# Two load buffers for the modulation weights, and a fourth for the blocks of w1, in a two-layer diffusion backbone

## The chip, the cores and the metric

The kernel runs on one core of one Trainium2 chip, as one launch. The metric is the device time of that launch in microseconds, the median of several runs. The engines of the core are TensorE (PE, with PEld for its weight loads), VectorE (DVE), ScalarE (ACT), GpSimd (POOL) and SyncE (SP), which issues nearly all DMAs here. The profile is one execution of the program; its clock starts at the first instruction.

## The reference, cut to what matters

512 latent tokens and 256 context tokens of width 1024 go through two layers. Each layer is a modulated norm, a mixer (Fourier, latent attention, convolution) with an output projection, and a squared-ReLU MLP of width 4096:

```python
def channel_mlp(h, l):
    return jnp.square(jax.nn.relu(h @ w_mlp1[l])) @ w_mlp2[l]

for l in range(DEPTH):
    last = l == DEPTH - 1
    mx = jnp.split((silu_c @ w_mod[l] + b_mod[l])[:, None, :], N_MOD, axis=-1)
    mc = jnp.split(silu_cc @ w_mod[l] + b_mod[l], N_MOD, axis=-1)
    ...
    if not last:
        ...
        hc = modulate(rms_norm(ctx, norm2_g[l]), mc[3], mc[4])
        ctx = ctx + mc[5] * channel_mlp(hc, l)
    x = x + mx[2] * mixer_rest(fx, gx, attn_x, l)
    hx = modulate(rms_norm(x, norm2_g[l]), mx[3], mx[4])
    x = x + mx[5] * channel_mlp(hx, l)
return rms_norm(x, final_norm_g)
```

The modulation (`mx` for the latent tokens, `mc` for the context) is a product of one vector with a 1024 x 6144 matrix for each layer and each of the two vectors. It doesn't depend on the tokens, so it can be worked out at any time before it is used. The change touches where the weights of that product are loaded while the MLP of layer 0 runs. The diff and the code call that layer 0 (`l == 0`); it is the first of the two, "layer one" in some speech.

## The kernel before, in words

**Products.** Activations lie with features on the 128 partitions and tokens on the free axis. Each fp32 operand is split in a high and a low part, and each product is three matmuls (`mm3`: high x high, high x low, low x high). Weights come by DMA into a raw buffer (tag `raw`), ACT makes the high part, and POOL or DVE subtracts to get the low part (`load_w`, tag `hl`, for whole 128 x 1024 tiles; `block`, tag `hs`, for 128 x 512 halves).

**The MLP.** Six of the 32 tiles of the hidden width are done plainly (`first_pairs`). The other 26 are done as 13 pairs (`pair(p)`, p = 3 to 15), whose latent part is a fast 2 x 2 scheme with seven half-size products (numbered 1, 6, 5, 7, 2, 3, 4 in the order of issue) in place of eight; the context part is four plain products. The sums of weight blocks that the scheme needs are DVE operations (L1183 to L1186), the sums of the products too (L1211), and then comes squared ReLU (L1169, L1044). After each pair, two blocks of w2 are multiplied with earlier hidden tiles: `downs` is called twice (j = 0 and j = 1), each with four output tiles mi = 0 to 3, and each output tile ends in an `update` (L983: one DVE operation for the latent part `resx`, one for the context part `resc`), which adds it to the residual. So one step of the loop in layer 0 is a pair and eight output tiles. PSUM holds three tiles for these in rotation (`ps` two, `pv` one) and two smaller ones (`tr`).

**The modulation.** Layer 0's last 8 groups of 128 outputs and all 48 of layer 1 are worked out on DVE during layer 0's MLP: `mod_group` loads 128 x 1024 weights (512 KB) into a buffer `w`, and one DVE reduce for each vector (`mj`, L274, with a short accumulator read behind it) multiplies it with the broadcast vector `c` and sums it. Layer 1's groups 0 to 15 need both vectors, so two reduces; groups 16 to 47 need one. Eight groups are spent in `first_pairs`; the other 48 are spent in the last call of `downs` of each step, four to a step in 12 steps: one ahead of the update of mi = 1, one ahead of that of mi = 2 and two ahead of that of mi = 3 (in the first of the steps, one, two and one). The first 16 of these 48 groups are the ones with two reduces. All 48 use one and the same buffer: `acc`, which is otherwise the accumulator of squares for the norms (and holds sums of `make_forms` early in the MLP).

**Order.** Each engine has one queue, in an order that is fixed when the program is built. The builder goes by the order in which the source emits instructions, but lets a later one pass where, by its own estimate of durations, an earlier one still lacks its inputs or its buffer. `tc.issue_after(mark[0])` keeps a reduce behind the DVE operation marked last (an update or a ReLU). So the reduces don't lie in the queues where the source emits them. A DMA that needs a buffer waits in SP's queue for the buffer's last reader, and everything behind it on SP waits too.

**Buffers.** Pool `ml` holds `raw` (128 x 1024 fp32, 4 KB on each partition, three buffers), `hs` (four of 4 KB) and `sw` (one of 6 KB). `raw` serves the blocks of w1 in both layers (`load_pair`), and by `wcfg` the tiles of the output projection and of the first tiles of w1. A pair takes two of the three. Pools are stacked in SBUF: after `ml` come, in layer 0, the broadcast vector `cb`, the buffers of the output projection's modulation (`mq`, `mr`, `mw`), and then the MLP's input `h2`.

Of the kernel before, what the change touches and what calls it, by code (L numbers as in the profile page):

```python
# [10 lines left out]
F32 = mybir.dt.float32  # L11
# [7 lines left out]
P = 128  # L19
D = 1024  # L20
# [54 lines left out]
def body(tc, A, out):  # L75
    nc = tc.nc
# [7 lines left out]
    def nm(s):  # L84
        cnt[0] += 1
        return f"{s}{cnt[0]}"

    def pool(name, **kw):
        cm = tc.tile_pool(name=nm(name), bufs=1, **kw)
        p = cm.__enter__()  # L90
        return p, lambda: cm.__exit__(None, None, None)

    cst, cst_close = pool("cst")
    wp, wp_close = pool("wp")
# [48 lines left out]
    wcfg = {"raw": [(wp, 2)], "hl": [(wp, 2)], "i": 0}  # L143
# [124 lines left out]
    def mod_group(o, w, l, g, nv=2):  # L268

        p, c, _ = o  # L270
        SY.dma_start(w, A["wmodT"][l, g])
        j = p.tile([P, D], BF16, tag="mj", name=nm("mj"), bufs=1)
        for v in range(nv):
            V.tensor_tensor_reduce(j, w, c[:, v], 1.0, vc("bmod", l, g), ALU.mult, ALU.add, mod[l][v][:, g:g + 1])  # L274
# [668 lines left out]
    for l in range(DEPTH):  # L943
# [7 lines left out]
        if l == 0:  # L951
            rx, rx_close = pool("rx")
            acc = rx.tile([P, D], F32, name="acc")
# [10 lines left out]
            load_res(0)  # L964
            load_res(1)
        ml, ml_close = pool("ml")
        wcfg.update(raw=[(ml, 3)], hl=[(wp, 2)], i=0)
        mods = None
        if l == 0:
            mods = open_mods()  # L970
# [8 lines left out]
        def update(pt, m, gate, cols, first, l=l):  # L979
            o0 = cols[0][0]  # L980
            for a, b, v in cols:
                r = res[v][m][:, a - S * v:b - S * v]
                mark[0] = V.scalar_tensor_tensor(r, pt[:, a - o0:b - o0],  # L983
                                                 mod[l][v][:, gate * 8 + m:gate * 8 + m + 1], r, ALU.mult, ALU.add).ins
                if first == "last":
                    sq_last[a, b] = tmp(b - a)
                    SC.activation(sq_last[a, b], r, AF.Square)
                elif first is not None:
                    add_square(acc[:, a:b], r, first)
# [58 lines left out]
        def more_mods(w):  # L1048
            ll, g = todo.pop(0)
            with tc.issue_after(mark[0]):  # L1050
                mod_group(mods, w, ll, g, 2 if ll == 0 or g < 16 else 1)
# [5 lines left out]
            return w  # L1057

        def load_pair(p, i):
            raw = ml.tile([P, 2, 512], F32, tag="raw", name=nm("raw"), bufs=3)  # L1060
            SY.dma_start(raw, A["w1"][l, 2 * p + i].rearrange("p (k n) -> p k n", k=2))
            return raw

        def load_tile(j):

            e = FIRST_W[l][j]
            if FIRST_AT[l][j] == "h":
                w = load_w(A["w1"][l, j], 1024, eng=e)
                return [w[:, :, 0:512], w[:, :, 512:1024]]
            raw = load_pair(j // 2, j % 2)  # L1070
            return [block(raw[:, i], e) for i in range(2)]
# [32 lines left out]
        def down(tiles, jobs, cols):  # L1104

            o0, nk = cols[0][0], len(tiles)
            os = sums_for(len(jobs), cols[-1][1] - o0)
            for (w, mi), o in zip(jobs, os):
                for k, ht in enumerate(tiles):
                    r = slice(k * (1024 // nk) + mi * P, k * (1024 // nk) + mi * P + P)  # L1110
                    mm3([(o[:, a - o0:b - o0], ht[:, 0, a:b], ht[:, 1, a:b]) for a, b, _ in cols],
                        w[:, 0, r], w[:, 1, r], k == 0, k == nk - 1)
            return os
# [59 lines left out]
        def pair(p):  # L1173


            ctx = not last
            r1, r2 = load_pair(p, 0), load_pair(p, 1)
            sw = ml.tile([P, 3, 512], F32, tag="sw", name=nm("sw"), bufs=1)
            hid[2 * p], hid[2 * p + 1] = ht = [unit(), unit()]
# [43 lines left out]
        def downs(ts, w, j, n):  # L1223
            for mi, o in enumerate(o for i in range(n) for o in down(ts, [(w, i)], whole)):
                if mods and len(hid) >= 8:
                    for _ in range(MODS[len(hid) > 8][j * n + mi]):
                        if todo:
                            more_mods(acc)
                update(o, j * n + mi, 5, whole, None)

        def load_down(j):
# [26 lines left out]
        for st in steps:  # L1258
            if isinstance(st, int):
                pair(st)  # L1260
                continue
            c, j = st
            for _ in range(plan.pop(0) if plan else 0):
                make_forms(made)
                made += 1
            ts = tiles(4 * c, 4) if last else tiles(2 * c, 2)
            downs(ts, ahead.pop(0) if ahead else load_down(8 // nd * c + j), j, nd)
# [179 lines left out]

# [10 lines left out]
```

## Time and profile before

| | |
|---|---|
| median of 3 runs | 1619.68 us |
| the runs | 1611.36, 1622.63, 1619.68 us |
| the profiled execution | 1613.05 us, span 1611.3 us |
| TensorE's mean granted clock | 0.983 of full speed |

The span is the time from the first to the last instruction on the core, so 1.75 us of the profiled execution lie around it. The profiled execution is 6.6 us shorter than the median of the runs, and the runs lie 11 us apart.

### The profile page before, as it was taken

The page shows a single profiled execution, that of the slowest core. Times are in us where ns is not written, and L with a number is a line of the kernel's source. Part 1 is how long each engine was busy: PE and PEld are TensorE (multiplying, and loading weights), DVE is VectorE, ACT ScalarE, POOL GpSimd, SP SyncE. Part 2 cuts the span into 40 slices and gives each one's busy share as a digit, 9 for nine tenths or more (in the row PEclk, how much of TensorE's full clock was granted, in tenths as well). Part 3 has the DMA queues.
Part 4 walks back from the last instruction along what each step waited for, and adds up shares of the span by engine and source line. Part 5 has one row for each costly group of instructions (what it writes and reads, how often), then busy time and mean ns, then how long its engine had stood idle before and what let it go on. Part 6 is the DMA issues. An engine that isn't in the chain of part 4 may idle for free.

```text
span 1611.3 us, 24743 instructions
## 1 busy us (share of the span) xinstructions
PE 1512.9 (94%) x9524; PEld 1322.3 (82%) x9524; DVE 1210.0 (75%) x1967; ACT 697.9 (43%) x1291; POOL 663.3 (41%) x440
## 2 busy tenths in 40 slices
PE   5998998899999999999999999899999989999997
PEld 3698877788888888889999987777878778888997
DVE  3489678867798899877877869978866676666655
ACT  3343577742423332333333244268854434444442
POOL 0034234212324554444454332443325566666671
PEclk9999999999999999999999999999999989999999
DMA  8331111066322333334333323100023122223321
GB/s 286 118 127 34 60 60 59 1 231 214 131 68 90 105 105 118 118 125 150 119 106 133 116 92 114 36 27 26 32 78 106 60 86 88 94 93 105 106 79 66
DMA packets 51142, 159.55 MB, mean 99 GB/s; under 512 B 5808, under 2 KB 13776, under 8 KB 50512
## 3 DMA queue, kind: packets, MB, share of 16 engines
q1 hardware_dynamic: 50592, 152.69, 28.7%
q0 software_dynamic: 432, 5.28, 0.8%
q8 instruction: 75, 1.23, 0.3%
q14 instruction: 43, 0.35, 0.1%
HBM read 155.84 MB, written 2.11 MB: 98 GB/s over the span
## 4 chain that ended last, share of the span: by engine, by line
PE 57%; DVE 22%; issue 6%; ACT 5%; DMA 5%; POOL 3%; DVEq 0%; SPq 0%; POOLq 0%; ACTq 0%
PE ps L160 30%; PE pv L160 15%; PE tr L160 6%; DVE mj L274 4%; DMA acc<-in_wmodT 3%; DVE aw L751 2%; ACT p L842 2%; DVE ac L751 2%; DVE resx L983 2%; PE tr L858 2%; PE po L160 1%; POOL hl L156 1%; PE tr L288 1%; PE p L160 1%; DVE t L1139 1%
## 5 line engine op out<-in xcount | busy, mean ns | idle before, releaser
L160 PE MATMUL ps<-y,hl 128*128 128x512 f32 (+1 forms) x2004 | 408.6, 356 | 8.2 <-DVE resc L983 3.8
L160 PEld LDWEIGHTS ps<-y,hl 128*128 128x128 f32 x2004 | 325.5, 189 | 70.5 <-DVE resc L983 7.5
L156 POOL TENSOR_TENSOR hl<-raw,hl 128x1024 fp32r<-128x1024 f32 (+1 forms) x90 | 223.4, 2483 | 252.2 <-ACT hl L155 252.1
L160 PE MATMUL pv<-y,hl 128*128 128x512 f32 (+1 forms) x1032 | 212.3, 355 | 1.9 <-DVE resc L983 1.7
L155 ACT ACTIVATE hl<-raw 128x1024 fp32r<-128x1024 f32 (+2 forms) x94 | 98.0, 1045 | 241.2 <-PE pv L160 112.2
L160 PEld LDWEIGHTS pv<-y,hl 128*128 128x128 f32 x1032 | 167.9, 188 | 34.2 <-DVE resc L983 3.1
L1056 POOL TENSOR_TENSOR hs<-raw,hs 128x512 fp32r<-128x512 f32 x95 | 133.2, 1404 | 125.2 <-ACT hs L1055 125.1
L160 PE MATMUL ps<-h,hs 128*128 128x256 f32 (+1 forms) x1080 | 151.4, 293 | 4.2 <-DVE t L1211 2.2
L1055 ACT ACTIVATE hs<-raw 128x512 fp32r<-128x512 f32 x133 | 82.9, 630 | 155.0 <-DMA raw<-in_w 42.3
L160 PEld LDWEIGHTS ps<-h,hs 128*128 128x128 f32 x1080 | 140.4, 193 | 10.1 <-issue 2.4
L983 DVE SCALAR_TENSOR_TENSOR resx<-ps,mod,resx 128x512 f32<-128x512 f32 (+1 forms) x134 | 95.6, 718 | 46.6 <-PE ps L160 46.6
L274 DVE CUSTOM_DVE_ANT_0 mj<-acc,cb,vec 128x1024 bf16<-128x1024 f32 x64 | 102.5, 1602 | 35.9 <-DMA acc<-in_wmodT 35.6
L1163 POOL TENSOR_TENSOR y<-t,y 128x256 fp32r<-128x256 f32 (+1 forms) x78 | 73.5, 956 | 113.6 <-DVE t L1169 110.0
L179 POOL TENSOR_TENSOR sm<-sm,mhalf 128x2 f32<-128x2 f32 (+2 forms) x16 | 17.7, 1109 | 193.8 <-DVE sm L177 193.8
L160 PE MATMUL tr<-h,hs 128*128 128x256 f32 x624 | 84.0, 285 | 0.0
L862 DVE TENSOR_TENSOR pT<-tr,pT 128x384 fp32r<-128x384 f32 (+1 forms) x144 | 74.0, 533 | 9.7 <-ACT pT L861 9.1
L861 ACT ACTIVATE pT<-tr 128x384 fp32r<-128x384 f32 (+1 forms) x144 | 65.8, 477 | 34.6 <-PE tr L858 33.5
L858 PE MATMUL tr<-ident,p 128*128 128x128 f32 x416 | 69.3, 281 | 11.1 <-DVE pT L862 7.0
L160 PEld LDWEIGHTS tr<-h,hs 128*128 128x128 f32 x624 | 79.3, 193 | 0.6
L983 DVE SCALAR_TENSOR_TENSOR resx<-pv,mod,resx 128x512 f32<-128x512 f32 (+1 forms) x75 | 54.0, 722 | 34.1 <-PE pv L160 33.9
L160 PE MATMUL pv<-h,hs 128*128 128x256 f32 (+1 forms) x504 | 77.4, 303 | 2.3 <-DVE h L225 2.3
L160 PEld LDWEIGHTS pv<-h,hs 128*128 128x128 f32 x504 | 69.4, 194 | 6.1 <-DVE h L225 2.7
(283 smaller groups left out, 2941.0 us busy)
## 6 DMA issues: line engine op xcount, KB each, us to landing
raw<-in_w SPq DMA_DIRECT2D x128, 512.0 KB, 3.6
acc<-in_wmodT SPq DMA_DIRECT2D x48, 512.0 KB, 3.5
mq<-in_wmods SPq DMA_DIRECT2D x32, 512.0 KB, 7.0
raw<-in_wo SPq DMA_DIRECT2D x17, 512.0 KB, 4.5
ztab<-in_dftx POOLq DMA_DIRECT2D x2, 2064.0 KB, 9.8
mw<-in_wmodT SPq DMA_DIRECT2D x8, 512.0 KB, 5.1
y<-in_wmodT SPq DMA_DIRECT2D x8, 512.0 KB, 5.5
raw<-in_win SPq DMA_DIRECT2D x8, 448.0 KB, 4.0
```

Of the source, the lines that this page charges most:

```text
L155: SC.activation(w[:, 0], raw, AF.Copy)
L156: side[eng].tensor_tensor(w[:, 1], raw, f(w[:, 0]), ALU.subtract)
L160: PE.matmul(o, lhsT=l, rhs=r, start=start, stop=stop)
L274: V.tensor_tensor_reduce(j, w, c[:, v], 1.0, vc("bmod", l, g), ALU.mult, ALU.add, mod[l][v][:, g:g + 1])
L751: V.scalar_tensor_tensor(acw[ct], us[ct][:, i:i + wide], vc("wdw", l, ct * TAPS + i), acw[ct], ALU.mult, ALU.add)
L858: PE.transpose(tr[:, (kt - ka) * P:(kt - ka + 1) * P], ptiles[i][:, kt * P:kt * P + P], ident)
L861: SC.activation(d[:, 0], src, AF.Copy)
L862: V.tensor_tensor(d[:, 1], src, f(d[:, 0]), ALU.subtract)
L983: mark[0] = V.scalar_tensor_tensor(r, pt[:, a - o0:b - o0], mod[l][v][:, gate * 8 + m:gate * 8 + m + 1], r, ALU.mult, ALU.add).ins
L1055: SC.activation(w[:, 0], src, AF.Copy)
L1056: side[eng].tensor_tensor(w[:, 1], src, f(w[:, 0]), ALU.subtract)
L1163: GP.tensor_tensor(ht[:, 1, a:a + n], src, f(ht[:, 0, a:a + n]), ALU.subtract)
```

## The change

Three things change. In `downs`, `mod_group` gets a tile of its own (tag `mw` in pool `ml`, two buffers of 4 KB on each partition) in place of `acc`. The tag `raw` of pool `ml` has four buffers in place of three, in both layers and for both users of the tag. The space that the build sets aside in SBUF for the descriptors of DMAs issued by GpSimd is halved, from 4096 to 2048. The pool `ml` grows by 4 KB in layer 1 and by 12 KB in layer 0, so what is stacked above it moves up by as much.

```diff
--- before.py
+++ after.py
@@ -964,7 +964,7 @@
             load_res(0)
             load_res(1)
         ml, ml_close = pool("ml")
-        wcfg.update(raw=[(ml, 3)], hl=[(wp, 2)], i=0)
+        wcfg.update(raw=[(ml, 4)], hl=[(wp, 2)], i=0)
         mods = None
         if l == 0:
             mods = open_mods()
@@ -1057,7 +1057,7 @@
             return w
 
         def load_pair(p, i):
-            raw = ml.tile([P, 2, 512], F32, tag="raw", name=nm("raw"), bufs=3)
+            raw = ml.tile([P, 2, 512], F32, tag="raw", name=nm("raw"), bufs=4)
             SY.dma_start(raw, A["w1"][l, 2 * p + i].rearrange("p (k n) -> p k n", k=2))
             return raw
 
@@ -1225,7 +1225,7 @@
                 if mods and len(hid) >= 8:
                     for _ in range(MODS[len(hid) > 8][j * n + mi]):
                         if todo:
-                            more_mods(acc)
+                            more_mods(ml.tile([P, D], F32, tag="mw", name=nm("mw"), bufs=2))
                 update(o, j * n + mi, 5, whole, None)
 
         def load_down(j):
@@ -1447,7 +1447,7 @@
 
 def kernel(**inputs):
     ins = _layout({k: np.asarray(v) for k, v in inputs.items()})
-    nc = bacc.Bacc("TRN2", target_bir_lowering=False, num_devices=1, dynamic_dma_scratch_size=4096)
+    nc = bacc.Bacc("TRN2", target_bir_lowering=False, num_devices=1, dynamic_dma_scratch_size=2048)
     aps = {n: nc.dram_tensor(f"in_{n}", a.shape, F32, kind="ExternalInput").ap() for n, a in ins.items()}
     out = nc.dram_tensor("out_y", (P, KT, S), F32, kind="ExternalOutput").ap()
     with tile.TileContext(nc) as tc:
```

## Rows read from the trace of the kernel before

**Rows 1.** The page: busy time, share of the span and instructions of each engine.

```profile
PE 1512.9 (94%) x9524; PEld 1322.3 (82%) x9524; DVE 1210.0 (75%) x1967; ACT 697.9 (43%) x1291; POOL 663.3 (41%) x440
```

**Rows 2.** Windows, one MLP step each: length, engines' busy time (instructions), clock, DMA, GB/s.

```profile
537.24:573.60 36.36, 33.47 (x230) 30.46 (x229) 33.06 (x51) 11.17 (x20) 16.85 (x11) 1.00 0.33 115
573.60:609.34 35.74, 33.47 (x231) 30.44 (x230) 32.28 (x52) 11.24 (x20) 17.52 (x11) 1.00 0.37 118
609.34:645.27 35.93, 33.46 (x231) 30.44 (x229) 32.41 (x52) 11.24 (x20) 17.50 (x11) 1.00 0.36 117
645.27:681.56 36.29, 33.78 (x230) 30.46 (x229) 32.87 (x52) 11.23 (x20) 17.52 (x11) 1.00 0.37 122
681.56:718.48 36.92, 34.56 (x230) 32.02 (x229) 27.55 (x43) 11.22 (x20) 14.88 (x11) 0.95 0.36 121
718.48:751.21 32.73, 32.73 (x230) 30.42 (x229) 26.06 (x43) 11.12 (x20) 15.25 (x11) 1.00 0.40 128
```

**Rows 3.** Timeline of PE: start, length, matmuls, [idle before, releaser].

```profile
651.01 1.59 PE L160 MATMUL pv<-y,hs 128*128 128x256 f32 x12
...
659.88 1.66 PE L160 MATMUL ps<-y,hs 128*128 128x256 f32 x12 [1.54 <-DVE t L1211]
...
670.07 2.38 PE L160 MATMUL ps<-y,hl 128*128 128x512 f32 x12 [0.77 <-DVE resc L983]
...
692.90 2.35 PE L160 MATMUL ps<-h,hs 128*128 128x256 f32 x12 [2.22 <-DVE t L1211]
695.05 2.45 PE L160 MATMUL tr<-h,hs 128*128 128x256 f32 x12
```

**Rows 4.** Timeline of DVE around the pair that starts at 645.27.

```profile
640.81 1.27 DVE L274 CUSTOM_DVE_ANT_0 mj<-acc,cb,vec 128x1024 bf16<-128x1024 f32 x1
...
642.67 1.27 DVE L274 CUSTOM_DVE_ANT_0 mj<-acc,cb,vec 128x1024 bf16<-128x1024 f32 x1
...
646.14 0.47 DVE L983 SCALAR_TENSOR_TENSOR resc<-pv,mod,resc 128x256 f32<-128x256 f32 x1
647.59 2.51 DVE L274 CUSTOM_DVE_ANT_0 mj<-acc,cb,vec 128x1024 bf16<-128x1024 f32 x1 [0.98 <-DMA acc<-in_wmodT]
...
656.57 1.28 DVE L274 CUSTOM_DVE_ANT_0 mj<-acc,cb,vec 128x1024 bf16<-128x1024 f32 x1 [2.34 <-DMA acc<-in_wmodT]
```

**Rows 5.** Waits between 537.24 and 718.48: who for whom, total, times, longest.

```profile
DVE mj L274 <- DMA acc<-in_wmodT: 16.7, 11, 2.5
```

**Rows 6.** Timeline of SP over the same step: DMA issues.

```profile
652.99 0.33 SPq L271 DMA_DIRECT2D acc<-in_wmodT  x1
653.41 2.00 SPq L1061 DMA_DIRECT2D raw<-in_w  x2
```

**Rows 7.** The tile `acc`: times from its DMAs' issue to their landing.

```profile
DMA to landing us min/median/max: 3.3/3.5/4.8
```

**Rows 8.** Timeline of POOL over the same step.

```profile
646.60 2.41 POOL L156 TENSOR_TENSOR hl<-raw,hl 128x1024 fp32r<-128x1024 f32 x1 [6.40 <-ACT hl L155]
```

**Rows 9.** Windows: output projection, first pairs (layer 0); MLP of layer 1.

```profile
340.00:420.00 80.00, 78.15 (x455) 65.20 (x454) 56.43 (x86) 23.75 (x38) 21.63 (x9) 0.98 0.68 241
420.00:500.00 80.00, 77.52 (x445) 67.07 (x444) 75.57 (x121) 27.37 (x45) 30.29 (x17) 1.00 0.24 81
1404.00:1468.00 64.00, 64.00 (x398) 57.20 (x397) 40.75 (x59) 27.01 (x45) 42.83 (x31) 1.00 0.30 99
```

**Rows 10.** Timeline of POOL around its own DMAs in layer 0.

```profile
108.28 0.53 POOL L583 DMA_DIRECT2D ctab<-in_dftc  x1
115.13 2.12 POOL L179 TENSOR_TENSOR sm<-sm,mhalf 128x6 f32<-128x6 f32 x1 [6.32 <-DVE sm L177]
```

**Rows 11.** The tile `ctab`: time from its DMA's issue to its landing.

```profile
DMA to landing us min/median/max: 11.0/11.0/11.0
```

**Rows 12.** Timelines: SP's issue of `mq`, and PE's first use of it.

```profile
339.12 1.91 SPq L280 DMA_DIRECT2D mq<-in_wmods  x4
...
351.06 1.92 PE L288 MATMUL tr<-mq,c 128*32 128x512 f32 x16
```

## The prediction, made before the changed kernel had run

> **What bounds the kernel now.** The page comes first: TensorE is busy 94% of the span and DVE 75% [rows 1]. Kernel-wide, then, there are some 100 us without matmuls, and the question is how many lie where the change works. For that I cut the MLP of layer 0 into steps, each from the first context product of a pair to that of the next pair [rows 2]. From 718.48 on a step takes 32.73 us and TensorE is busy for all of it; the two steps behind it look the same, and so does the one ahead of the stretch. That is the floor that TensorE sets. The five steps from 537.24 to 718.48 take 36.36, 35.74, 35.93, 36.29 and 36.92 us, together 181.24. Against five times 32.73 = 163.65 that is 17.6 us too much: 13.4 in the first four (the ones with two reduces to a group), 4.2 in the fifth.
>
> Who holds TensorE up there? In the timeline of PE each of the first four steps has two stops, one for a sum of products on DVE (1.54 us) and one for an update on DVE (0.77) [rows 3]; the fifth has one of 2.22, behind which two lots of 12 matmuls take 2.35 and 2.45 us, where such a lot takes 1.59: 1.6 us more. The granted clock of that step is 0.95, of the others 1.00 [rows 2], so for a while after the stop it was at the lower of its two levels, 1.2 GHz. And what holds DVE? It is busy 32.3 to 33.1 us of each of the first four steps [rows 2]. Within a step it stops twice, for the weights of a modulation group: 0.98 and 2.34 us [rows 4]; over the five steps that is 16.7 us in 11 waits [rows 5]. The reason is the single buffer: its next load can't be issued before the last reduce has read it (643.94 for the reduce of 642.67), and it lands some 3.5 us later [rows 7].
>
> So there the bound is DVE plus its waits for loads; everywhere else in the loop it is TensorE.
>
> **The change part by part.**
>
> *Two buffers for the modulation.* No instruction is added: 48 loads and 64 reduces as before. With two buffers, groups 1 and 2 of a step can be loaded as soon as groups 3 and 4 of the step before are read, so their waits go. The loads of groups 3 and 4 leave when 1 and 2 have been read. With the rows at hand: T is the start of the pair (645.27). Group 1 is read from 640.81 to 643.94, and group 3 lands at 643.94 + 3.5 = 647.4. Group 2 (now from 647.59) moves up behind group 1: two reduces of 1.27 and two updates between them of 0.75 + 0.47 = 1.2 each, which ends near 649, and group 3 is there by then. Thus 3.3 us of waiting per step are gone. What is late next? DVE's own work, 32.28 to 33.06 us a step, mean 32.65 [rows 2], which is TensorE's floor of 32.73 almost to the tenth. Two engines that are both full seldom fit without friction. In a step at the floor, DVE still stands idle for 32.73 - 26.06 = 6.7 us, most of it because TensorE isn't ready for it. So below, the first four steps gain between nothing (the reduces get in TensorE's way elsewhere) and 13.4. Part of the friction is paid back: the second group's reduce takes 2.51 us beside a POOL subtract of 2.41 [rows 4, 8], and earlier, in POOL's pause of 6.40 us, such a reduce takes 1.27. I take about 1 us of friction a step, 13.4 - 4 = 9.4, since the mean of DVE's busy time is nearest to the floor. The fifth step has only 27.55 us of DVE work, so it should fall to the floor whole: 4.2. Sum 13.6. The seven later steps are at the floor and gain nothing; their four reduces (one to a group) close up too, and DVE's 6.7 us of slack cover that. Without that cover each microsecond that TensorE waits would cost one, seven times over.
>
> *SP's queue.* All these loads wait in one queue. Now the two loads of the next pair's w1 stand behind a load of `acc` (652.99, then 653.41) [rows 6]; with a free buffer they are issued sooner. They serve a pair that starts at 681.56, some 28 us later, so this is worth nothing, and the load of a group that now goes early is 512 KB on queues that are a third busy [rows 2].
>
> *The fourth raw buffer.* In layer 1's MLP TensorE is busy 64.00 of 64.00 us [rows 9], so blocks that come sooner save nothing; what hides it is that full queue. In the output projection and first pairs of layer 0 TensorE stands idle for 1.85 and 2.48 us [rows 9]: a gain of at most 4.3, though the stops there are mostly for DVE. On the other side, a load of 512 KB that goes sooner at the 241 GB/s of that stretch takes 2.2 us from those of `mq`, which are issued from 339.12 on and used at 351.06 [rows 12]; the bound of the loss is 2.2. I take 0, since the larger part of that idle time isn't for loads.
>
> *The smaller descriptor space, and the addresses.* GpSimd issues three DMAs in all. If half the space held it until the one of 108.28 has landed, 11.0 us later, at 119.3 [rows 10, 11], the operation of 115.13 would be 4.2 us late, and TensorE waits for that one. Nothing in the trace shows such a hold, POOL's pause there being a wait for DVE: between 0 and +4.2, I take 0. That pools move up by 12 KB changes which old tile a first load waits for; the nearest row is again `mq`, whose loads come 12 us ahead of use, so I take 0 and keep 2.2 as the bound.
>
> **Sum.** 1613.05 - 13.6 = 1599.4 against the profiled execution. The median of the runs is 6.6 us above that execution, and the runs lie 11 us apart, so about 1% is what can be told from no change. On the median: 1619.7 - 13.6 = **1606 us**.
>
> **The rivals.**
>
> *All of it comes back.* The reduces move out of POOL's way and DVE's work falls to some 30 us a step: two reduces of 1.2 us less each. Then all five steps reach the floor: -17.6, and up to 4 more from the start of the MLP: 1598 to 1602 us. For it speaks the reduce of 1.27 us at 640.81, in POOL's pause; against it that groups 3 and 4 then fall where POOL works again.
>
> *The wait becomes work.* DVE has no slack in the four steps, and the second stop is for an update that is late because of two reduces and a ReLU ahead of it, not for a load alone. If friction is 2 us or more a step, 4 to 8 us stay: 1612 to 1616. To this belongs the case that the change does not do what it says, since SP serves in order: a load of w2 that waits for POOL, put ahead of a group's load, holds that as the single buffer did.
> By the Trainium skill (Perfetto Trace Analysis, Identifying the Most-Contended Engine) occupancy names the bottleneck, and DVE's 75% beside TensorE's 94% would say that DVE's waits cost nothing: 1620 us. The steps of this trace say otherwise (DVE 33.06 of 36.36 us), so I give that reading a twentieth.
>
> *The reduces bunch up, and it is slower.* Place: the end of `downs` and the start of a pair. Now the missing load of group 2 lets the last update pass (it ends at 646.6, T + 1.3) [rows 4]. Once loads are there, the builder may put all eight reduces ahead of it. From 640.81 that is 8 x 1.27 + 3 updates of 1.2 = 13.8 us, to T + 9.3. The PSUM tile of that update is wanted by product 5, at 651.01 = T + 5.7 [rows 3]. That is the deciding point: an update that ends later than T + 5.7 stops TensorE, here for 3.6 us, and two reduces beside POOL (2.4 in place of 1.27) make it 5.9. Against the 3.4 us lost now that is +2.5 a step, and a stop of that length may bring the lower clock, as the one of 2.22 did, for another 1.6 us [rows 3]: 4 x 4.1 = +16.4, less the 4.2 of the fifth step, and for the seven later ones (4 x 1.27 + 3.6 = 8.7 us, to T + 4.2, or T + 6.5 beside POOL) +0.8 each: together near +18, 1638 us. Against it: between the two reduces of a group another operation passes already (0.6 us lie between the end of the one of 640.81 and 642.67, and an update's first half runs there), which brings the last update in before T + 5.
> The Trainium skill (SBUF — State Buffer, Who interferes with whom) says that a DVE operation with two SBUF inputs and a GpSimd operation that reads SBUF lock each other out for a whole instruction. By that rule every moved reduce that meets POOL costs what the one of 2.51 us cost; the trace agrees with the rule in that one (POOL holds until 649.01, and 1.42 + 1.27 is near 2.51).
>
> **How the numbers follow.** Forecast, a gain of 9 to 16 us around 1606: 0.45. All comes back, 1600: 0.20. Wait becomes work or nothing happens, 1612 to 1620: 0.22, with the twentieth in it. Bunched, 1620 to 1638: 0.13. Faster by over 1% means below 1603.5: the second case and a little of the first, 0.25. Slower by over 1% means above 1635.9: half of the last case, 0.06. The rest, 0.69, lies within. The range: 1597 (all comes back, with the start of the MLP) to 1627 (the price of GpSimd's DMAs and of `mq`, 4.2 + 2.2, with no gain, or the bunched case half paid). The likeliest case's own is 1603 to 1611.
>
> **What would show it.** Right: in the changed trace DVE's waits for the modulation's weights fall from 16.7 us in the five steps to under 4; the steps fall to 33 to 34 us, the fifth to 32.7; the stops for L1211 and L983 shrink; the seven later steps and layer 1's MLP stay. Wrong: steps that stay at 36 us with DVE at 33 and no such waits (work, not waits); a stop of TensorE at product 5 and a lower clock behind it (bunching); waits for `mw` that stay (SP's order); or a difference outside this stretch, say a POOL stop behind its own DMAs, which the sum prices at nothing.

## The result: slower by 0.9%

The changed kernel takes 1630.1 us (median of 6 runs, 1623.7 to 1632.3) against 1614.2 (median of 6): a ratio of 1.0088, 95% interval 1.0067 to 1.0109. That is 24 us above the forecast of 1606 and outside the range. The forecast was a gain of 13.6 on a median of 1619.7 from three runs; with three more runs that median is 1614.2, so the measured loss is 15.9. The profiled execution took 1623.73 us, the fastest of the six; its span is 10.7 us longer than that of the profile of before.

Cut at the same places as before, the profile after loses in three stages and gains in one. The table is read from the timelines of PE: *projection* runs from the last product that reads `pT` in layer 0's attention to the first MLP product, *first pairs* from there to the first product of the loop, *ten steps* are the five steps of [rows 2] and the five behind them, and the layer 1 columns run from the last product that reads `pT` there to the first product that reads `ft`, and from that to the last one. All runs of the study stand in it, since the experiments below are read off the same columns. *Ratio* is to the runs of the kernel before on the same chip; the chips differ from one lot of experiments to the next. The stages are those of one execution each.

| kernel (median us; ratio, 95% interval) | projection | first pairs | ten steps | layer 1: projection, first pairs | layer 1: loop |
|---|---|---|---|---|---|
| before (1614.2) | 74.1 | 92.6 | 345.3 | 103.1 | 274.5 |
| **changed** (1630.1; 1.0088, 1.0067 to 1.0109) | 79.6 | 94.6 | 341.9 | 106.4 | 280.1 |
| mw only (1621.7; 1.0054, 1.0034 to 1.0073) | 83.1 | 92.5 | 342.5 | 102.9 | 275.8 |
| raw 4 only (1630.1; 1.0104, 1.0087 to 1.0121) | 79.4 | 94.6 | 342.6 | 106.8 | 280.5 |
| changed, raw 4 in layer 0 alone (1619.9; 1.0045, 1.0024 to 1.0066) | 79.7 | 96.2 | 341.2 | 103.0 | 274.0 |
| space only (1614.7; 1.0013, 0.9995 to 1.0030) | 74.1 | 92.5 | 344.4 | 102.3 | 276.0 |
| own pool (1612.1; 0.9989, 0.9972 to 1.0006) | 77.2 | 92.6 | 342.8 | 103.1 | 275.3 |
| after the update (1625.7; 1.0068, 1.0046 to 1.0090) | 79.6 | 92.1 | 357.7 | 103.1 | 274.3 |
| spread (1612.3; 0.9985, 0.9972 to 0.9999) | 74.7 | 92.5 | 342.3 | 102.3 | 275.0 |
| changed, order in layer 1 (1621.9; 1.0047, 1.0033 to 1.0061) | 80.8 | 96.2 | 341.2 | 106.6 | 273.9 |
| own pool, even (1610.1; 0.9988, 0.9967 to 1.0009) | 77.0 | 91.0 | 343.1 | 103.0 | 274.5 |
| spread, even (1619.1; 1.0030, 1.0014 to 1.0046) | 76.7 | 93.6 | 349.0 | 103.0 | 273.9 |
| before, even (1610.6; 0.9978, 0.9962 to 0.9994) | 74.5 | 93.8 | 345.8 | 102.9 | 275.2 |
| changed, even (1625.4; 1.0065, 1.0043 to 1.0087) | 80.8 | 96.2 | 337.5 | 105.8 | 281.1 |
| fourth apart (1607.9; 0.9968, 0.9951 to 0.9986) | 74.4 | 94.1 | 341.9 | 102.3 | 275.0 |
| fourth apart, even (1610.0; 0.9967, 0.9946 to 0.9987) | 74.5 | 94.5 | 337.6 | 102.3 | 275.5 |
| **fourth in the loop, even** (1604.8; 0.9946, 0.9928 to 0.9963) | 75.7 | 92.6 | 338.7 | 103.1 | 274.2 |

Changed less before: +5.5, +2.0, -3.4, +3.3, +5.6, together +13.0. The rest of the 10.7 is in the two mixers, which came out 1.5 and 1.0 us shorter in this execution; they vary so from run to run (the last read of `pT` in layer 0 lies between 333.6 and 339.2 us over the 17 profiles).

**The loop of layer 0.** Windows of the changed kernel, one step each, which answer to [rows 2]:

```profile
543.25:579.69 36.44, 34.40 (x231) 31.99 (x229) 33.12 (x52) 11.20 (x20) 14.46 (x11) 0.95 0.36 117
579.69:616.12 36.43, 34.39 (x230) 31.99 (x229) 33.27 (x52) 11.20 (x20) 14.72 (x11) 0.95 0.37 115
616.12:651.67 35.55, 33.16 (x231) 30.56 (x229) 32.44 (x52) 11.20 (x20) 14.39 (x11) 1.00 0.37 119
651.67:688.10 36.43, 34.39 (x230) 31.98 (x229) 33.07 (x53) 11.01 (x20) 15.29 (x11) 0.95 0.38 127
688.10:720.72 32.62, 32.62 (x230) 30.42 (x229) 27.14 (x43) 11.13 (x20) 15.91 (x11) 1.00 0.42 128
720.72:753.63 32.91, 32.91 (x231) 30.48 (x229) 27.60 (x43) 11.12 (x20) 15.83 (x11) 1.00 0.40 130
```

The fifth step falls to the floor, from 36.92 to 32.62, as forecast (with the kernel before it varies: 34.45 in the run with the smaller space alone). The first four stay where they were: 144.85 us in place of 144.32. The waits of DVE in those five steps, which answer to [rows 5], tell why:

```profile
DVE resx L983 <- PE ps L160: 8.6, 9, 1.0
DVE resx L983 <- PE pv L160: 4.8, 5, 1.0
...
DVE mj L274 <- DMA mw<-in_wmodT: 1.1, 1, 1.1
```

The waits for the weights are gone, 16.7 us to 1.1. But DVE now reaches its updates ahead of TensorE and stands there, with the next reduce queued behind the update: 8.6 + 4.8 = 13.4 us. The kernel before has, in the same two lines:

```profile
DVE resx L983 <- PE ps L160: 2.6, 3, 1.0
DVE resx L983 <- PE pv L160: 2.1, 3, 1.0
```

One wait took the place of the other: in the first four steps DVE is idle for 13.7 us before and 13.0 after (length less busy time). Then the reduces pile up. The timeline of DVE around the pair that starts at T = 651.67, which answers to [rows 4]:

```profile
652.11 1.27 DVE L274 CUSTOM_DVE_ANT_0 mj<-mw,cb,vec 128x1024 bf16<-128x1024 f32 x1
...
653.71 3.02 DVE L274 CUSTOM_DVE_ANT_0 mj<-mw,cb,vec 128x1024 bf16<-128x1024 f32 x1
...
657.33 1.93 DVE L274 CUSTOM_DVE_ANT_0 mj<-mw,cb,vec 128x1024 bf16<-128x1024 f32 x1
...
659.20 0.47 DVE L983 SCALAR_TENSOR_TENSOR resc<-pv,mod,resc 128x256 f32<-128x256 f32 x1
```

The last update ends at 659.67, T + 8.0; before, it ended at T + 1.3. In the timeline of PE (which answers to [rows 3]) the product that wants its PSUM tile waits for it, in all four steps and at the same place:

```profile
657.40 0.28 PE L160 MATMUL ps<-h,hs 128*128 128x256 f32 x1
659.73 2.20 PE L160 MATMUL pv<-y,hs 128*128 128x256 f32 x12 [2.04 <-DVE resc L983]
```

TensorE was free at 657.69, T + 6.0. The two stops of the kernel before (1.54 and 0.77) have become one of 2.04, and in three of the four steps the mean granted clock falls to 0.95. POOL's split at that time:

```profile
653.00 2.65 POOL L156 TENSOR_TENSOR hl<-raw,hl 128x1024 fp32r<-128x1024 f32 x1 [6.03 <-ACT hl L155]
```

The reduce that starts at 653.71 beside it takes 3.02 us; alone it takes 1.27. POOL is done at 655.65, and 1.94 + 1.27 = 3.21 would be a full lock-out. The rule cited in the prediction (the Trainium skill, SBUF — State Buffer, Who interferes with whom) agrees again, to 0.2 us. Moving the reduces out of one split of POOL's moved them into the next: the 35 reduces take 56.1 us in all, 57.7 before.

**The projection of layer 0.** Windows over the same slice, first of the kernel before, then of the changed one (columns as in [rows 2]):

```profile
350.00:360.00 10.00, 10.00 (x63) 7.31 (x62) 8.80 (x11) 2.48 (x4) 3.46 (x1) 1.00 0.83 296
```

```profile
350.00:360.00 10.00, 5.94 (x38) 3.43 (x31) 8.79 (x14) 2.59 (x4) 3.22 (x1) 1.00 0.88 324
```

TensorE loses 4.1 us here, in three stops. The timelines of ACT and PE in the changed kernel name a load of `wo` for the two longer ones; the first, of 0.80, is for `mr`, a copy in the modulation:

```profile
354.06 1.06 ACT L155 ACTIVATE hl<-raw 128x1024 fp32r<-128x1024 f32 x1 [1.84 <-DMA raw<-in_wo]
364.69 1.06 ACT L155 ACTIVATE hl<-raw 128x1024 fp32r<-128x1024 f32 x1 [9.57 <-DMA raw<-in_wo]
```

```profile
352.27 1.05 PE L160 MATMUL tr<-sel,mr 128*128 128x2 f32 x8 [0.80 <-ACT mr L291]
355.17 0.97 PE L160 MATMUL ps<-y,hl 128*128 128x512 f32 x4 [1.85 <-ACT hl L155]
...
358.52 1.67 PE L160 MATMUL ps<-y,hl 128*128 128x512 f32 x8 [1.41 <-POOL hl L156]
```

SP's timeline shows it queued elsewhere. Before:

```profile
335.23 0.43 SPq L151 DMA_DIRECT2D raw<-in_wo  x1
...
336.65 0.43 SPq L151 DMA_DIRECT2D raw<-in_wo  x1
```

Changed:

```profile
337.60 2.58 SPq L280 DMA_DIRECT2D mq<-in_wmods  x4
340.23 1.56 SPq L271 DMA_DIRECT2D mw<-in_wmodT  x2
341.89 0.50 SPq L151 DMA_DIRECT2D raw<-in_wo  x1
...
359.96 1.23 SPq L151 DMA_DIRECT2D raw<-in_wo  x2
```

The next two loads of `wo` now stand behind six loads of modulation weights, the second of them behind twelve. Before, both were issued ahead of the last product that reads `pT` (337.98); now both come behind it (336.47).

**Layer 1's MLP.** Its steps took 21.29 us (a few 21.6); now eleven of twelve take 21.9, each with a stop of 0.37 us or a little more. PE in the changed kernel, then DVE there, then DVE in the kernel before:

```profile
1376.95 1.67 PE L160 MATMUL ps<-h,hs 128*128 128x256 f32 x12 [0.37 <-DVE t L1211]
```

```profile
1374.86 1.61 DVE L1183 TENSOR_TENSOR sw<-raw 128x512 f32<-128x512 f32 x1
1376.39 0.41 DVE L1211 TENSOR_TENSOR t<-ps,t 128x256 f32<-128x256 f32 x1
1376.73 1.43 DVE L1184 TENSOR_TENSOR sw<-sw,raw 128x512 f32<-128x512 f32 x1
```

```profile
1368.95 1.27 DVE L1211 TENSOR_TENSOR t<-ps,t 128x256 f32<-128x256 f32 x3
1373.04 0.69 DVE L1183 TENSOR_TENSOR sw<-raw 128x512 f32<-128x512 f32 x1 [2.82 <-DMA raw<-in_w]
```

Before, the sum of the next pair's blocks (L1183) came behind three sums of products, because its block came late. With a fourth buffer the block is there, the sum stands in DVE's queue ahead of those that free TensorE's PSUM tiles, and it takes 1.61 us where it took 0.69.

### The profile page after: what moved, and what is told of

It is laid out like the page before. It is cut to its first block, busy times and chain, and to the rows that moved or that the text cites. A ratio compares the mean times of both kernels' runs of the same rounds, so it can differ in the third digit from the quotient of the medians.

```text
span 1622.0 us, 24704 instructions
## 1 busy us (share of the span) xinstructions
PE 1516.7 (94%) x9524; PEld 1327.0 (82%) x9524; DVE 1222.6 (75%) x1967; ACT 698.1 (43%) x1291; POOL 663.8 (41%) x440
## 4 chain that ended last, share of the span: by engine, by line
PE 44%; DVE 7%; issue 4%; ACT 4%; POOL 2%; DMA 1%; DVEq 0%; POOLq 0%; ACTq 0%; SPq 0%
PE ps L160 25%; PE pv L160 12%; PE tr L160 5%; DVE hs L1056 1%; ACT p L842 1%; POOL hl L156 1%; DVE t L1139 1%; DVE mj L274 1%; PE po L160 1%; PE tr L858 1%; DVE p L847 1%; ACT hs L1055 0%; ACT pT L861 0%; DVE sm L840 0%; ACT p L845 0%
## 5 line engine op out<-in xcount | busy, mean ns | idle before, releaser
L1056 POOL TENSOR_TENSOR hs<-raw,hs 128x512 fp32r<-128x512 f32 x95 | 144.5, 1522 | 101.7 <-ACT hs L1055 101.0
L160 PE MATMUL ps<-h,hs 128*128 128x256 f32 (+1 forms) x1080 | 156.4, 295 | 5.4 <-DVE t L1211 2.7
L274 DVE CUSTOM_DVE_ANT_0 mj<-mw,cb,vec 128x1024 bf16<-128x1024 f32 x80 | 124.8, 1560 | 13.7 <-DMA mw<-in_wmodT 13.4
```

What stands on the lines that cost most here:

```text
L160: PE.matmul(o, lhsT=l, rhs=r, start=start, stop=stop)
L1056: side[eng].tensor_tensor(w[:, 1], src, f(w[:, 0]), ALU.subtract)
```

## The experiments

Three causes were put to the test first, each with a part of the change.

**The two modulation buffers alone** (the changed kernel, less the fourth raw buffer):

```diff
-        wcfg.update(raw=[(ml, 4)], hl=[(wp, 2)], i=0)
+        wcfg.update(raw=[(ml, 3)], hl=[(wp, 2)], i=0)
-            raw = ml.tile([P, 2, 512], F32, tag="raw", name=nm("raw"), bufs=4)
+            raw = ml.tile([P, 2, 512], F32, tag="raw", name=nm("raw"), bufs=3)
```

> The two buffers for the modulation and the smaller descriptor space, with three raw buffers as before. Theory (three separate losses: reduces bunch in layer 0's loop, a grown pool delays loads of wo in layer 0's projection, the fourth raw buffer reorders DVE in layer 1's MLP): the four two-reduce steps stay near 36.2 us with one stop of 2 us at product 5, the fifth falls to 32.7, layer 0's projection still loses some 5 us, layer 1's steps go back to 21.4 us: about 5 us over the kernel before, 1619 us. Rival (the fourth raw buffer is behind all of it): the projection's loss and the stop at product 5 go as well, 1600 to 1606 us. Rival (descriptor space or addresses): 1625 to 1630 us as the changed kernel.

1621.7 us. Layer 1 is back (275.8), the four steps are at 36 us with the same stop of 2.04, the projection is as long as in the changed kernel or longer (83.1; the clock of its slice fell to 0.69). The fourth buffer is not behind all of it.

**The fourth raw buffer alone** (the modulation stays in `acc`):

```diff
-                            more_mods(ml.tile([P, D], F32, tag="mw", name=nm("mw"), bufs=2))
+                            more_mods(acc)
```

> The fourth raw buffer and the smaller descriptor space; the modulation's weights stay in the single buffer. Theory of three losses: the projection loses some 5 us (the pool has grown here too), the five steps keep their 181 us and their waits for acc, layer 1's steps are 21.9 us (+6): about 1627 us. Rival (the mw buffers are behind the loss): 1614 us, layer 1 at 21.4.

1630.1 us, as slow as the whole change. Layer 1 and both projections are as expected. A miss: the five steps are 177.2 us, not 181, and the ten 342.6, where the kernel before has 345.3 and the run with the smaller space alone 344.4, though DVE still waits for `acc`.

**Four raw buffers in layer 0, three in layer 1:**

```diff
-        wcfg.update(raw=[(ml, 4)], hl=[(wp, 2)], i=0)
+        wcfg.update(raw=[(ml, 4 if l == 0 else 3)], hl=[(wp, 2)], i=0)
-            raw = ml.tile([P, 2, 512], F32, tag="raw", name=nm("raw"), bufs=4)
+            raw = ml.tile([P, 2, 512], F32, tag="raw", name=nm("raw"), bufs=4 if l == 0 else 3)
```

> As the changed kernel, but four raw buffers in layer 0 alone and three in layer 1. Theory: layer 1's steps go back to 21.4 us, all else as in the changed kernel: some 6 us under it, 1623 us. Rival (what slows layer 1 is the weights' address or another state left by layer 0): layer 1 stays at 21.9, 1630 us.

1619.9 us, 10 under the changed kernel. Both layer 1 columns go back, the loop (274.0) and the projection (103.0), so the fourth buffer costs layer 1 some 9 us. I had counted the loop only. In the projection, ACT's line of the changed kernel shows how: a block's copy waits for w1 with the copy for `wo` queued behind it. The rows behind it are PE's, in the changed kernel and before: the stop grows from 0.54 to 2.21 us, and the same 46 matmuls take 1.35 longer.

```profile
1216.39 0.63 ACT L1055 ACTIVATE hs<-raw 128x512 fp32r<-128x512 f32 x1 [5.35 <-DMA raw<-in_w]
1216.93 1.04 ACT L155 ACTIVATE hl<-raw 128x1024 fp32r<-128x1024 f32 x1
```

```profile
1220.74 7.13 PE L160 MATMUL ps<-y,hl 128*128 128x256 f32 x46 [2.21 <-POOL hl L156]
```

```profile
1216.90 5.78 PE L160 MATMUL ps<-y,hl 128*128 128x256 f32 x46 [0.54 <-POOL hl L156]
```

**The smaller descriptor space alone:**

```diff
-    nc = bacc.Bacc("TRN2", target_bir_lowering=False, num_devices=1, dynamic_dma_scratch_size=4096)
+    nc = bacc.Bacc("TRN2", target_bir_lowering=False, num_devices=1, dynamic_dma_scratch_size=2048)
```

> The kernel before with the smaller descriptor space alone, which also moves all pools down by 2 KB. Theory: no change, 1614 us within 0.3%, layer 0's projection as before. Rival (the space or the addresses cost): 4 us or more, 1618 us and up, with the stretch from ctab's load at 108.28 or the projection longer.

No change. It moves every pool by 2 KB, and the loads of `wo` still go ahead of those of `mq`.

**A pool of their own for the two buffers**, opened behind the projection, and three raw buffers:

```diff
+        if mods:
+            mdp, mdp_close = pool("mdp")
         h2t = [h2p.tile([P, 2, nq], F32R, name=nm("h2")) for _ in range(KT)]
...
-                            more_mods(ml.tile([P, D], F32, tag="mw", name=nm("mw"), bufs=2))
+                            more_mods(mdp.tile([P, D], F32, tag="mw", name=nm("mw"), bufs=2))
```

> The two buffers for the modulation in a pool of their own, opened behind the projection, and three raw buffers: the pool that holds the blocks has its old size and ends below the attention's pT again. Theory (the projection's loss comes from the grown pool lying over pT, which holds up the loads of wo): TensorE is busy for 10.0 of 10.0 us in the slice 350 to 360 again, layer 0's MLP starts near 412 us, the five steps stay near 177 us with the stop at product 5: about 1610 us. Rival (the loads of the modulation themselves cost the projection): 1619 to 1622 us as with the two buffers in the blocks' pool.

1612.1 us. TensorE is busy for 10.00 of 10.00 us in the slice from 350 on. In the addresses of the built programs the blocks' pool ended, before, on the very byte of a partition at which `pT` begins (109,312); it reaches 4 KB into `pT` with the fourth raw buffer, 8 KB with the two `mw`, 12 KB with both. In the six programs where it reaches in, TensorE is busy for 5.9 to 8.2 us of that slice; in the other eleven for 10.0. The part of the expectation on the start of the MLP (412) was missed: it starts at 416.4, after 77.2 us of projection. Here TensorE loses its time late, with a stop of 0.98 us for ACT at 407.60 and a clock of 0.90 between 400 and 420. Three more kernels with the old pool size lose 2.6 to 5.5 us behind a full slice (after the update, own pool even, spread even: 79.6, 77.0 and 76.7 us); why was not settled. So the effect of the pool's size is read from the slice, and the column of the table holds more than that effect.

**Reduces behind the update** in place of ahead of it, the rest as above:

```diff
+                update(o, j * n + mi, 5, whole, None)
                 if mods and len(hid) >= 8:
                     for _ in range(MODS[len(hid) > 8][j * n + mi]):
                         if todo:
                             more_mods(mdp.tile([P, D], F32, tag="mw", name=nm("mw"), bufs=2))
-                update(o, j * n + mi, 5, whole, None)
```

> As the own pool, and each group's reduces are issued behind the update of the output tile that they stood ahead of. Theory (the stop at product 5 is an update that bunched reduces delay): the stop of 2 us goes, the four two-reduce steps fall to 33 to 34.5 us: 1600 to 1604 us. Rival (DVE is full, whatever the order): the stop moves to another sum and the steps stay near 36 us: 1610 us.

1625.7 us, a clear miss. The stop at product 5 is gone, and three others are there: the reduces now stand ahead of the sums of products (L1213 is L1211 of the other kernels). DVE, then PE:

```profile
543.36 2.15 DVE L274 CUSTOM_DVE_ANT_0 mj<-mw,cb,vec 128x1024 bf16<-128x1024 f32 x1
...
546.04 2.37 DVE L274 CUSTOM_DVE_ANT_0 mj<-mw,cb,vec 128x1024 bf16<-128x1024 f32 x1
...
548.35 0.41 DVE L1213 TENSOR_TENSOR t<-ps,t 128x256 f32<-128x256 f32 x1
```

```profile
548.90 1.66 PE L160 MATMUL ps<-h,hs 128*128 128x256 f32 x12 [1.29 <-DVE t L1213]
```

It hits the later steps too, which have half the reduces: 35.0 to 35.7 us in place of 32.7 to 33.0.

**One group at every second output tile:**

```diff
-MODS = ((0, 0, 0, 0, 0, 1, 2, 1), (0, 0, 0, 0, 0, 1, 1, 2))
+MODS = ((0, 1, 0, 1, 0, 1, 0, 1), (0, 1, 0, 1, 0, 1, 0, 1))
```

> As the own pool, with a step's four groups spread over its eight output tiles (one at every second tile) in place of four at the last three. Theory: no update stands behind more than two reduces, the stop of 2 us goes or shrinks below 1 us, steps of 33 to 34.5 us: 1600 to 1604 us. Rival (loads of the early groups then come late, or DVE is full): waits for mw or stops at the output tiles, steps near 36 us: 1610 us.

1612.3 us: the rival's time. At product 5 one stop of 0.41 is left, in the first step; but there is one of 2.6 to 2.8 at an output tile in each of three steps. From the fifth step on all are on the floor, 32.62 each. The step ahead of the ten, 32.6 in the kernels that don't spread the groups, is 3.0 longer, so the column of the ten steps flatters this run (and the next one with the spread, where that step takes 34.45).

```profile
602.77 3.52 PE L160 MATMUL pv<-y,hl 128*128 128x512 f32 x12 [2.66 <-DVE resc L983]
```

**The old order of the sums in layer 1**, in the changed kernel:

```diff
-            V.tensor_tensor(sw[:, 0], r2[:, 0], r2[:, 1], ALU.add)
+            with tc.issue_after(fourth[0]) if last and fourth[0] is not None else nullcontext():
+                V.tensor_tensor(sw[:, 0], r2[:, 0], r2[:, 1], ALU.add)
...
-                        V.tensor_tensor(d, o[j], x, ALU.add)
+                        i_ = V.tensor_tensor(d, o[j], x, ALU.add).ins
+                        if name == "v":
+                            fourth[0] = i_
```

> The changed kernel, with one edge added in layer 1's pairs: the first sum of the next pair's blocks is issued behind the fourth sum of products of this pair, as it stood before the change. Theory (layer 1's steps are longer because that sum, whose block now comes early, goes ahead of the sums of products that free PSUM): steps of 21.3 to 21.4 us, no stops of 0.4 us for L1211: 1624 us. Rival (the earlier loads or blocks cost by themselves): steps stay at 21.9 us, 1630 us.

1621.9 us. All twelve steps take 21.28 or 21.29 us, the stops are gone, and one row shows that order alone does it: the sum of the blocks (here L1187) still takes long, 1.81 us, behind the three sums of products (here L1215).

```profile
1378.44 1.35 DVE L1215 TENSOR_TENSOR t<-ps,t 128x256 f32<-128x256 f32 x3
1379.71 1.81 DVE L1187 TENSOR_TENSOR sw<-raw 128x512 f32<-128x512 f32 x1
```

**An even order of the groups.** Eight reduces in a step were too many at any place, so the next four runs give every step 5 or 6: the 16 groups with two reduces go to all twelve steps.

```diff
-        todo = [(0, g) for g in range(40, 48)] + [(1, g) for g in range(48)] if mods else []
+        two, one = iter(range(16)), iter(range(16, 48))
+        todo = [(0, g) for g in range(40, 48)] + [(1, next(two if c == "2" else one)) for c in "211212111121" * 4] if mods else []
```

With the own pool:

> The own pool for the two buffers, and the order of the groups changed: the 16 groups with two reduces go to all twelve steps of the loop (one or two in each, so 5 or 6 reduces a step) in place of the first four (8 a step). Theory (the stop at product 5 comes when the bunched reduces end the last update later than the start of a pair + 5.7 us): with two or three reduces fewer that update ends some 3 us sooner, near +5, the stop goes in all steps, all steps 32.7 to 33.2 us: 1597 to 1600 us. Rival (any bunch at the end of a step stops TensorE): each of twelve steps gets a stop of about 1 us, 1612 us and more.

With the spread:

> The spread over the eight output tiles and the even order of groups together, two buffers in their own pool. Theory (spread reduces stop TensorE at the output tiles where two follow each other, by 2.7 us in a step of four such pairs): steps with one or two such pairs are at 32.7 to 33.5 us: 1596 to 1602 us. Rival (a single pair of reduces at an output tile already stops TensorE): stops of 1 us or more in all twelve steps, 1608 to 1615 us.

In the kernel before, with its single buffer:

> The kernel before (one buffer, three raw buffers) with the even order of groups alone. Theory (where DVE has 2 to 4 us of slack in a step, its waits for the single buffer cost nothing): all steps 32.7 to 33.5 us although the waits for acc stay at some 3 us a step: 1598 to 1602 us. Rival (the waits themselves hold TensorE's sums): the stop for L1211 stays at 1 us or more in each of twelve steps, 1612 us or more.

In the changed kernel:

> The changed kernel with the even order of groups alone. Theory: the stop at product 5 goes here too, some 13 us less in the four steps; the longer projections and layer 1's steps of 21.9 us stay: 1616 us. Rival (the fourth raw buffer changes layer 0's loop): stops stay, 1626 to 1630 us.

All four expectations were too low: 1610.1, 1619.1, 1610.6 and 1625.4 us. The stop of 2.04 is gone from the own pool's steps (what is left at product 5 is 0.3 to 0.5 in two of them), which fits an update that is late because of the reduces ahead of it. But the loss does not go with it: steps of 33.0 to 35.6 us, most of them over the floor, where six had been at or near it. The single buffer with even groups takes as long as two buffers (1610.6 and 1610.1). Only with the fourth raw buffer (last run) does the loop get shorter, 337.5 us. Two of its steps as windows, and behind them the two stops of such a step in PE's timeline:

```profile
547.52:581.56 34.04, 33.24 (x231) 30.59 (x229) 30.37 (x47) 11.12 (x20) 16.61 (x11) 1.00 0.41 135
581.56:614.18 32.62, 32.62 (x231) 30.42 (x229) 27.12 (x46) 11.13 (x20) 16.77 (x11) 1.00 0.37 130
```

```profile
555.71 1.45 PE L160 MATMUL ps<-h,hs 128*128 128x256 f32 x10 [0.62 <-DVE hs L1057]
557.34 1.67 PE L160 MATMUL ps<-h,hs 128*128 128x256 f32 x12 [0.19 <-DVE t L1212]
```

**The fourth raw buffer in the late pool**, so that it serves layer 0 and the blocks' pool keeps its size:

```diff
+            if mods and len(hid) >= PLAIN and i and p % 2:
+                raw = mdp.tile([P, 2, 512], F32, tag="raw4", name=nm("raw"), bufs=1)
+            else:
+                raw = ml.tile([P, 2, 512], F32, tag="raw", name=nm("raw"), bufs=3)
```

> Two modulation buffers and layer 0's fourth raw buffer in a pool of their own behind the projection (first pairs and loop), three raw buffers in layer 1; the blocks' pool keeps its old size; groups in their old order. Theory (the pool's size costs the projection, not the fourth buffer): from the last read of pT to the start of the MLP 74 to 77 us, not 79.5 to 81; first pairs 92.5 if the pool's size was behind their loss too; loop as in the run with four buffers in layer 0 alone, 176.8 us in the five steps: 1610 us. Rival (the fourth buffer itself, loaded early, delays the loads of wo): 79 us and more, first pairs 94.6 to 96.2: 1617 to 1620 us.

With the even order:

> The same with the even order of groups. Theory (fourth buffer and even order together shorten layer 0's loop, and the projection pays nothing once the pool keeps its size): ten steps of 337 to 338 us in place of 345.3, projection 74 to 77 us: 1604 to 1607 us, under both kernels. Rival (the loop's gain in the changed kernel with even order was from something else in it): loop at 343 us, 1610 us.

With the even order, for the loop alone (the condition is `mods and p > 2 and i and p % 2`):

> The same with the even order, but the fourth raw buffer serves the loop's pairs alone, not the first pairs. Theory (early blocks cost the first pairs something): first pairs 92.5 us or less, loop 337 to 338 us: 1603 to 1606 us. Rival (the first pairs' loss was the pool's place): first pairs the same in both of the last two runs.

1607.9, 1610.0 and 1604.8 us. The projection takes 74.4 to 75.7 us in all three: what lengthened it was the pool's size, not the buffer. (The plainest pair is the two `mw` in the blocks' pool and in their own, with the same buffers: 7.22 and 10.00 us of the slice.) The first pairs are 1.5 to 2 us longer with the fourth buffer in the first two and 92.6 in the third; but there they have the same stops for updates (0.58, 0.76, 0.98 and 0.76 us) as in the first (0.59, 0.76, 0.94, 0.76), and their first 32 matmuls happened to take 7.71 us in place of 9.26. So that the first pairs are spared is not shown. The loop is at 341.9 with the old order, 337.6 and 338.7 with the even one; in the last kernel one step has a stop of 2.25 at product 5, behind a load of `mw` that DVE waits 2.82 us for. That kernel, at 0.9946 (0.9928 to 0.9963), beats the kernel before clear of its interval; the intervals of these three overlap, so the order among them is not shown.

## Why the prediction was wrong, step by step

- **DVE's waits for the single buffer go:** right. 16.7 us became 1.1.
- **Four steps gain 9.4:** wrong, they lost 0.5. The step that failed is the one that set DVE's busy time (32.65) beside TensorE's floor (32.73) and priced the friction at 1 us a step. DVE's queue has a fixed order: a wait that ends at one instruction came back at the next ones that must wait for TensorE (4.7 us in five steps before, 13.4 after), and the reduces behind them were late just the same. Busy time alone left no room for such waits in the sum: of DVE's 13.0 us of idle time in the four steps after, some 12 are waits for TensorE.
- **The fifth step gains 4.2:** right in this execution, 4.30. **The later steps gain nothing:** right (164.1 and 164.5 in five).
- **The bunching rival**, given 0.13: right in its place (product 5 in all four steps), its point (the update ended at T + 8.0, TensorE was free at T + 6.0) and the lower clock (three of four). Its price was too high: the stop is 2.04, not 3.6 to 5.9, since six reduces, not all eight, got ahead of the last update. It cost what the old stops had cost, so the four steps broke even. Slower it became elsewhere; that the measured 1630 lies in this rival's range (1620 to 1638) is luck.
- **The rival in which the wait becomes work or nothing happens** (0.22) describes the four steps best, in its outcome. The reading beside it (the Trainium skill, Perfetto Trace Analysis, Identifying the Most-Contended Engine) would have DVE's waits cost nothing; their removal did bring nothing there, yet not for want of a bound on DVE: it is the releaser of every stop.
- **Addresses, 0 with a bound of 2.2:** wrong, and the largest step in layer 0: +5.5. I bounded it by `mq`, the load that I took for the nearest. The loads that the grown pool held up were mainly those of `wo`, and the place to look at was where the pool ended: on the first byte of `pT`. That the size decides is shown by the slice from 350 in seventeen programs; that it is `pT` and no other tile is read from the addresses.
- **The fourth raw buffer, 0 in layer 1 ("what hides it is that full queue"):** wrong by 8.9 us, 5.6 in the loop and 3.3 ahead of it. TensorE was busy for 64.00 of 64.00 us, which says that an earlier block can't help. It doesn't say that it can't hurt: the late block had kept a DVE sum behind more urgent ones, and an edge that puts it back there gives the whole 5.6 back.
- **First pairs, between -4.3 and +2.2, taken 0:** +2.0, within the bounds. It goes with the fourth buffer. In PE's timeline the kernel before has three stops for updates there (0.37, 0.37 and 0.97 us), the changed one four (0.64, 0.76, 0.96 and 0.73), which is 1.4 of the 2.0; which instruction makes the updates late was not settled.
- **Descriptor space, 0:** right.

The fourth raw buffer also shortens layer 0's loop, which the prediction did not look at: by 4.5 to 5.6 us with the even order (343.1 against 337.5, 337.6 and 338.7) and by 1 with the old one (342.8 against 341.9), when the even order alone does nothing. The traces show where. With two `mw` and three raw buffers, DVE waits for a block of w1 in six of the ten steps; with the fourth buffer in none. The own pool with the even order: all these waits, the one of the third step (601.75 to 637.11), and PE's stops behind it in that step:

```profile
DVE sw L1186 <- DMA raw<-in_w: 13.8, 6, 2.9
```

```profile
616.47 0.69 DVE L1186 TENSOR_TENSOR sw<-raw 128x512 f32<-128x512 f32 x1 [2.86 <-DMA raw<-in_w]
```

```profile
621.42 2.39 PE L160 MATMUL pv<-y,hl 128*128 128x512 f32 x12 [0.56 <-DVE t L1214]
...
626.47 2.37 PE L160 MATMUL ps<-y,hl 128*128 128x512 f32 x12 [0.56 <-DVE resc L983]
```

The same step of the changed kernel with the even order has neither that wait nor these two stops, and takes 34.06 us in place of 35.36. Over the ten steps TensorE's stops sum to 10.0 us in the first and 5.3 in the second. With the old order the six waits (13.3 us) lie in the later steps, and only three stops of 0.25 to 0.55 us follow them. That these waits are the whole of the difference is not shown.

## What to carry to other kernels

An engine that is full in a trace is a reason why a change there gains nothing, and no reason why it costs nothing: where instructions queue in order, a buffer that makes something early also puts it ahead of something urgent, so list what it will pass. Before a pool grows, look at which older tile lies behind its last byte; one opened later, behind that tile's last use, can hold the addition without that loss. And where a wait for a load is removed on an engine that also waits for the bottleneck, count the second wait before booking the first as a gain.

## What the runs showed of the hardware

The same stop of 2.04 us at product 5 lowered the clock in some steps and not in others. With the own pool, the first two steps as windows:

```profile
541.55:577.09 35.54, 33.14 (x230) 30.54 (x229) 32.78 (x52) 11.20 (x20) 14.72 (x11) 1.00 0.36 119
577.09:613.52 36.43, 34.39 (x230) 31.99 (x229) 32.88 (x52) 11.20 (x20) 14.64 (x11) 0.95 0.34 116
```

The next two repeat them. The counts of matmuls and the stop are the same; at the lower clock TensorE is busy for 1.25 us longer, and a later stop of 0.36 for DVE, which the steps at full clock have, is gone. So the lower clock costs 0.9 us a step; what decides between the two is not shown. And small stops cost more than they show: the step with 0.62 + 0.19 = 0.81 us of idle time is 1.42 us longer than its neighbour, which has none, since TensorE is also busy for 0.62 us longer (33.24 against 32.62) at the same clock of 1.00.
